# Region tiles and weight-split buffers start 0, 16, 32 or 48 bytes into their homes

## The chip, the cores and the metric

The kernel runs on one core of one Trainium2 chip. The metric is the device time in microseconds (us). The time of the kernel before is 2475.23 us, the median of 2 runs (2475.09 to 2475.36).

## What is computed

Two transformer blocks on 256 tokens of width 2048, all in float32 (the reference cut to its spine; the norms are RMS norms with a gain):

```python
def first_block(x, mem, ...):                      # x, mem: [1, 256, 2048]
    h = x
    h = h + hybrid_mixer(rms_norm(h, norm_mix), w_in, ..., w_out)      # w_in 2048 x 8272, w_out 2048 x 2048
    h = h + memory_cross_attention(rms_norm(h, norm_cross), rms_norm(mem, mem_norm), wq, wk, wv, wo, ...)
    h = h + sqrelu_mlp(rms_norm(h, norm_mlp), w_up, w_down)            # 2048 x 8192, 8192 x 2048
    return h

def hybrid_mixer(xn, w_in, ...):
    hq, hf, hi, hg, aq, ak, av, iq, ik, iw = split(xn @ w_in)
    y_h = hgrn2_group(hq, hf, hi, hg, ...)         # gated recurrence, 8 heads of 128
    y_a = dsa_group(aq, ak, av, iq, ik, iw, ...)   # top-64 causal attention, 8 heads of 128
    return concat(y_h, y_a) @ w_out

def sqrelu_mlp(hn, w_up, w_down):
    return square(relu(hn @ w_up)) @ w_down

def second_block(x, ...):
    x = x + neighbourhood_attention(rms_norm(x, ...), na_w_qkv, ..., na_w_o)   # 2048 x 6144, 2048 x 2048
    return x + sqrelu_mlp(rms_norm(x, ...), mlp_w1, mlp_w2)                    # 2048 x 8192, 8192 x 2048
```

## The kernel before

Every large product streams a weight matrix from HBM once. The stream is cut into chunks of 128 partitions x 1024 float32, two row tiles of 512 columns each. For a chunk, `emit_dma` loads `raw` on SP's queue (4 buffers); `emit_split` splits it exactly into two float32r parts: ScalarE (ACT) copies `raw` to `hi` (L374), VectorE (DVE) writes `lo = raw - hi` (L375); both have 4 buffers (`SPLIT_BUFS`), used in turn. The activations are split in the same way, so each product takes three matmuls: high x high, high x low, low x high. `emit_mm` issues them in one of two forms:

- **Transposed blocks** (`tr=True`, L408: the first part of the mixer's input projection and both up projections). The weights are stationary: 128 columns of `hi` or `lo` are loaded into TensorE, and 256 tokens of the activations `xT_hi` or `xT_lo` move through it. The output is feature by token.
- **Token blocks** (L415, L416, L417: all others). 128 tokens of the activations are stationary and 512 columns of `hi` or `lo` move (256 columns for the cross attention's values, `wv_x`). The activations are `xT_hi`/`xT_lo` for projections from the residual, and pairs of region tiles (`r` in the trace) for projections from something computed: the mixer's and the attentions' outputs, the normed memory, the squared ReLU.

A matmul with operands of float32r takes one weight load (LDWEIGHTS, on the row PEld of the trace) and one MATMUL (on PE). Nearly every matmul has a load of its own, and a trace shows the load of the next matmul begin when the present matmul begins.

Large intermediates live in nine regions of 8192 bytes per partition, made by `region(i, shape)` in pool `reg`: r0 to r7 of `[P, 8, 256]` or `[P, 2, 1024]`, and r8. Later stages take the same homes again: in the MLPs, group `g` of up columns uses r(2(g%4)) for its high and r(2(g%4)+1) for its low part; the neighbourhood attention keeps q and k in r0 to r3, v in r8 and its output in r4 to r7; the mixer's output lies in r0, r4, r5 and r6. Residual `X`, `xT_hi`, `xT_lo` and the identity (`cst`) are in pool `const`, and their addresses are not touched by any of these calls.

Work beside the stream (evacuations, softmax, the recurrence) is written as generators in lanes. Python clocks with estimated costs decide where in the program each of its steps goes; these clocks know sizes, not addresses.

GpSimd (POOL) issues 43 DMAs, among them two for each of the 16 bias tables (`relraw`) of the neighbourhood attention. The descriptors of these go through a scratch area at the start of SBUF, 16384 bytes per partition by default.

Addresses: the pools lie one behind the other, and every home is a multiple of 32 bytes. In the program as built, the first bytes of the operands of TensorE, modulo 64, are these (columns of 128 or 512 elements inside a tile are whole multiples of 64 bytes further on):

```
tile                         before   after
xT_hi, xT_lo, X, cst            0       0
raw (4 buffers)                32      32
hi, lo (buffers 0, 1, 2, 3)    32      32, 48, 0, 16
r0, r1                         32      32
r2, r3                         32      48
r4, r5                         32       0
r6, r7                         32      16
r8, wA, wE, wB                 32      32
```

Of the kernel before, what the change touches and what calls it, by code (L numbers as in the profile page):

```python
# [13 lines left out]
F32R = mybir.dt.float32r  # L14
# [8 lines left out]
P = 128  # L23
# [11 lines left out]
# columns of the transposed table of gains  # L35
# [20 lines left out]
class Block:  # L56
    """One block of output columns: w[kts, cols] against the stationary activations."""
# [7 lines left out]
class Act:  # L65
    """Transposed activations, each value split exactly into two float32r parts."""
# [9 lines left out]
def block_kernel(ctx: ExitStack, tc: "_tile.TileContext", a: dict, out: bass.AP, phases=ALL_PHASES):  # L76
# [27 lines left out]
    def region(i, shape, dtype=F32):  # L104
        return reg.tile(shape, dtype, tag=f"r{i}", name=nm(f"r{i}"))

    # ------------------------------------------------------------------ lanes of side work
    # Work beside the stream of weights is written as generators, each in a lane. The estimated clocks
    # below only order the program: a stage goes out when the one before it should be done by the time
    # the tensor engine gets there, and when ACT and DVE aren't too far behind it.  # L110
# [102 lines left out]
    # ------------------------------------------------------------------ constants  # L213
# [19 lines left out]
    # ------------------------------------------------------------------ small arithmetic  # L233
    def rsqrt(lane, x, n, mul=1.0, out=None):
        """1/sqrt(x) * mul of a [P, n] tile: an integer first guess, then Newton's steps."""
# [17 lines left out]
    def make_rstd(lane, key, ss, want_sq=False):  # L253
        """ss: [P, 2 * 4] sums of squares, one per token half and column block."""
        v = vec
        m = st(f"mr{lane}", 2)
        v.tensor_reduce(m, ss.rearrange("p (t c) -> p t c", t=2), axis=AX.X, op=ALU.add)
        ms = const.tile([P, 2], F32, name=nm("ms"))
        v.tensor_scalar(ms, m, 1.0 / D, EPS, op0=ALU.mult, op1=ALU.add)
        if want_sq:  # L260
            r2 = const.tile([P, 2], F32, name=nm("rsq"))
            v.reciprocal(r2, ms)
            rstd_sq[key] = r2
        else:
            rstd[key] = rsqrt(lane, ms, 2, out=const.tile([P, 2], F32, name=nm("rstd")))
        mark(("rstd", key))
# [3 lines left out]
    def build_half(lane, ver, cb, gain, half):  # L270
        """Two feature tiles of the finished residual: transposed, with the gain, split in two."""
# [43 lines left out]
    def split_act(hi, lo, src, scale=None):  # L315
        """hi + lo = src * scale, exactly; src in PSUM or SBUF."""
# [9 lines left out]
    def product(dst, l, r, first=True, last=True):  # L326
        """dst (+)= l^T r; operands split in two parts take three products."""
# [10 lines left out]
    def split_gains(parts, ps, gains):  # L338
        """The same of two feature tiles in one PSUM bank, each with its own gain."""
# [6 lines left out]
    # ------------------------------------------------------------------ the stream of weights  # L346
    plan = []

# [21 lines left out]
    def emit_split(c):  # L370
        n = len(c.kts) * c.block.width
        c.hi = stream.tile([P, 1024], F32R, tag="hi", name=nm("hi"))
        c.lo = stream.tile([P, 1024], F32R, tag="lo", name=nm("lo"))
# [53 lines left out]
    # ------------------------------------------------------------------ evacuations  # L427
    def ev_tokens(dst, key, after=None):
        """dst[tt] = projection * rstd, one row per token."""
# [13 lines left out]
    def ev_heads(dstT, key, gain, after, mul=1.0, lane="E", factor=None):  # L443
        """Four heads of 128: RMS norm of each, transposed; dstT(pair) is [128, 2, 256].

        With factor, the norm is left to the scores: factor["ss"] holds the heads' sums of squares.
        """
# [61 lines left out]
    def softmax_rows(lane, groups, factor=None):  # L509
        """groups: (scores [P, n, w] in SBUF or PSUM, destination [P, n, w]); normalised rows.  # L510

        factor(group) is a [P, n] of positive factors that the scores still lack.
        """
# [72 lines left out]
    # ------------------------------------------------------------------ phase: mixer  # L586
    def mixer():
# [46 lines left out]
        # --- indexer  # L634
# [91 lines left out]
        # --- sparse attention heads  # L726
# [70 lines left out]
        # --- gated recurrence heads  # L797
# [78 lines left out]
        def levels(g, pl):  # L876
            """Scores of the recurrence, S^T[s, t] = sum_k q[t] k[s] prod(f, s < . <= t): pairs are met at
            the level where a block of 2b tokens holds s in its left and t in its right half; q carries the
            products from its half's start, k those to its half's end."""
# [47 lines left out]
            def right_pairs(b, ps):  # L927
                """The level's products, for the tokens in right halves alone."""
# [95 lines left out]
    # ------------------------------------------------------------------ attention of dense heads  # L1024
    def probs_pair(qT, kTt, h0, pT, keys, bias=None, lane="A", pl="A", factor=None):
        """Two heads: softmax(q k^T + bias), transposed into the two tiles pT()."""
# [42 lines left out]
    def values_pair(pT, V, vcol, oT_hi, oT_lo, oh, act_o, vkey):  # L1069
        """out^T of two heads from their transposed probabilities, split into the next operand."""  # L1070
# [14 lines left out]
    # ------------------------------------------------------------------ phase: cross attention  # L1085
# [98 lines left out]
    # ------------------------------------------------------------------ phase: squared-ReLU MLP  # L1184
# [47 lines left out]
    # ------------------------------------------------------------------ phase: neighbourhood attention  # L1232
# [85 lines left out]
    # ------------------------------------------------------------------ the program  # L1318
# [107 lines left out]
```

## Time and profile before

| | |
|---|---|
| time, median of 2 runs | 2475.23 us |
| span of the profiled execution | 2475.9 us |
| PE busy | 2459.3 us, 99% of the span, 14885 matmuls |
| PEld busy | 2186.8 us, 88% |
| DVE busy | 1455.8 us, 59% |
| ACT busy | 1136.8 us, 46% |
| POOL busy | 169.5 us, 7% |
| DMA queue of SP | 440.19 MB, 57.0% of 16 engines |

How to read it: a matmul's busy time runs from its start to its modelled end and overlaps that of the next one, so 99% only says that PE is never without work. What one matmul costs in a stream is the distance from its start to the next one's start. The profile gives it in two ways: starts in the view in order of time, and the chain of work that ended last, whose merged pieces give the time of a run of matmuls together with their count.

### The profile page before, as it was taken

To read this page: it belongs to the slowest core of one execution; us is meant where nothing else is said; L and a number is where in the kernel's file an instruction comes from. 1 tells how busy PE (TensorE), PEld (TensorE's weight loads), DVE (VectorE), ACT (ScalarE), POOL (GpSimd) and SP (SyncE) were. 2 spreads that over 40 slices of the span, in tenths; PEclk is the share of its full clock that TensorE was granted. 3 is DMA by queue.
4 is the path that set the end of the run, shared out by engine and by line. 5 is a ranking of instruction groups with operands and counts; after the bars stand their busy time and mean duration, and the time that the engine had idled before them with its cause. 6 is when DMAs were issued, how large, how long until landed. Compare 5 with 4: busy or idle time off the path is not lost.

```text
span 2475.9 us, 36932 instructions
## 1 busy us (share of the span) xinstructions
PE 2459.3 (99%) x14885; PEld 2186.8 (88%) x14885; DVE 1455.8 (59%) x1719; ACT 1136.8 (46%) x1465; POOL 169.5 (7%) x345
## 2 busy tenths in 40 slices
PE   8999999999999999999999999999999999999999
PEld 8779998888998899899898888888998899899897
DVE  5575666665655555555556566666655555555554
ACT  5455533465543444444444554554543444444443
POOL 1020012211000000000000312230000000000000
PEclk9999999999999999999999999999999999999999
DMA  7555545555556556566655656555556656566654
GB/s 225 162 172 161 151 145 156 193 177 167 170 178 198 193 182 194 187 194 191 189 187 174 196 169 179 167 186 180 179 180 195 195 180 196 188 194 188 190 187 167
DMA packets 235644, 449.40 MB, mean 182 GB/s; under 512 B 16321, under 2 KB 21057, under 8 KB 235473
## 3 DMA queue, kind: packets, MB, share of 16 engines
q1 hardware_dynamic: 232528, 440.19, 57.0%
q0 software_dynamic: 2368, 5.80, 1.0%
q8 instruction: 116, 1.90, 0.3%
q10 hardware_dynamic: 576, 1.05, 0.1%
q14 instruction: 56, 0.45, 0.1%
HBM read 444.83 MB, written 2.10 MB: 181 GB/s over the span
## 4 chain that ended last, share of the span: by engine, by line
PE 95%; POOL 1%; DMA 1%; DVE 1%; ACT 1%; issue 0%; SPq 0%; ACTq 0%; POOLq 0%; DVEq 0%
PE acc L408 34%; PE acc L415 19%; PE acc L416 19%; PE acc L417 19%; PE sdA L157 3%; PE sdE L157 2%; DMA raw<-in_w_in_dram 1%; DMA relraw<-in_rel_dram 0%; POOL rhB L157 0%; ACT hi L374 0%; DVE lo L375 0%; DMA wA<-in_mem_dram 0%; POOL rhD L157 0%; DVE wB L157 0%; POOL rhE L157 0%
## 5 line engine op out<-in xcount | busy, mean ns | idle before, releaser
L375 DVE TENSOR_TENSOR lo<-raw,hi 128x1024 fp32r<-128x1024 f32 (+1 forms) x835 | 1005.1, 1222 | 495.0 <-ACT hi L374 492.0
L374 ACT ACTIVATE hi<-raw 128x1024 fp32r<-128x1024 f32 (+1 forms) x835 | 867.7, 1056 | 799.5 <-PE acc L417 406.0
L408 PE MATMUL acc<-xT_hi,hi 128*128 128x256 f32 x2448 | 690.6, 282 | 0.0
L408 PE MATMUL acc<-xT_hi,lo 128*128 128x256 f32 x2448 | 688.3, 281 | 0.1
L408 PE MATMUL acc<-xT_lo,hi 128*128 128x256 f32 x2448 | 688.2, 281 | 0.0
L415 PE MATMUL acc<-hi,r 128*128 128x512 f32 (+1 forms) x1408 | 543.6, 386 | 0.7 <-ACT r L157 0.7
L417 PE MATMUL acc<-hi,r 128*128 128x512 f32 (+1 forms) x1408 | 541.5, 385 | 0.0
L416 PE MATMUL acc<-lo,r 128*128 128x512 f32 (+1 forms) x1408 | 541.4, 384 | 0.0
L408 PEld LDWEIGHTS acc<-xT_lo,hi 128*128 128x128 f32 x2448 | 461.2, 188 | 0.6
L408 PEld LDWEIGHTS acc<-xT_hi,hi 128*128 128x128 f32 x2448 | 461.2, 188 | 0.6
L408 PEld LDWEIGHTS acc<-xT_hi,lo 128*128 128x128 f32 x2448 | 461.2, 188 | 0.3 <-DVE lo L375 0.3
L417 PEld LDWEIGHTS acc<-hi,r 128*128 128x128 f32 x1408 | 264.5, 188 | 53.1 <-DVE r L157 0.4
L415 PEld LDWEIGHTS acc<-hi,r 128*128 128x128 f32 x1408 | 264.7, 188 | 52.3 <-ACT r L157 1.1
L416 PEld LDWEIGHTS acc<-lo,r 128*128 128x128 f32 x1408 | 264.7, 188 | 51.0
L415 PE MATMUL acc<-hi,xT_hi 128*128 128x512 f32 x736 | 295.0, 401 | 0.0
L416 PE MATMUL acc<-lo,xT_hi 128*128 128x512 f32 x736 | 290.9, 395 | 1.4 <-DVE lo L375 1.4
L417 PE MATMUL acc<-hi,xT_lo 128*128 128x512 f32 x736 | 290.5, 395 | 0.0
L157 DVE SCALAR_TENSOR_TENSOR X<-acc,rsq,X 128x512 f32<-128x512 f32 x128 | 96.1, 751 | 147.0 <-PE acc L417 147.0
L415 PEld LDWEIGHTS acc<-hi,xT_hi 128*128 128x128 f32 x736 | 138.1, 188 | 33.8 <-issue 2.7
L417 PEld LDWEIGHTS acc<-hi,xT_lo 128*128 128x128 f32 x736 | 137.9, 187 | 33.7
L416 PEld LDWEIGHTS acc<-lo,xT_hi 128*128 128x128 f32 x736 | 138.2, 188 | 32.7 <-DVE lo L375 1.9
L157 DVE SCALAR_TENSOR_TENSOR wE<-acc,wE 128x512 f32<-128x512 f32 x64 | 44.3, 692 | 109.2 <-ACT wE L157 108.6
(175 smaller groups left out, 1121.9 us busy)
## 6 DMA issues: line engine op xcount, KB each, us to landing
raw<-in_mlp_w_dram SPq DMA_DIRECT2D x256, 512.0 KB, 4.2
raw<-in_w_up_dram SPq DMA_DIRECT2D x128, 512.0 KB, 3.9
raw<-in_w_down_dram SPq DMA_DIRECT2D x128, 512.0 KB, 4.3
raw<-in_w_in_dram SPq DMA_DIRECT2D x127, 512.0 KB, 3.9
raw<-in_na_w_qkv_dram SPq DMA_DIRECT2D x96, 512.0 KB, 4.2
raw<-in_w_out_dram SPq DMA_DIRECT2D x32, 512.0 KB, 4.2
raw<-in_na_w_o_dram SPq DMA_DIRECT2D x32, 512.0 KB, 4.1
raw<-in_wk_x_dram SPq DMA_DIRECT2D x8, 512.0 KB, 4.4
```

What stands on the lines that cost most here:

```text
L157: return f(*args, **kw)
L374: nc.scalar.activation(c.hi[:, :n], c.raw[:, :n], AF.Copy)
L375: nc.vector.tensor_tensor(c.lo[:, :n], c.raw[:, :n], c.hi[:, :n], op=ALU.subtract)
L408: nc.tensor.matmul(dst, l, r, start=first and i == 0 and o == 0, stop=last and i == 2, skip_group_check=True,)
L415: nc.tensor.matmul(dst, h, wh, start=first, stop=False)
L416: nc.tensor.matmul(dst, h, wl, start=False, stop=False)
L417: nc.tensor.matmul(dst, l, wh, start=False, stop=last)
```

## The change

`region` no longer makes a tile of the wanted shape; it takes a flat tile of 2064 elements (8256 bytes) and returns a view that begins `4 * (i // 2)` elements into it, so 0 bytes for r0 and r1, 16 for r2 and r3, 32 for r4 and r5, 48 for r6 and r7, and 0 for r8. `emit_split` takes tiles of 1040 elements (4160 bytes) and begins 0, 16, 32 or 48 bytes into them, by a counter that goes round with the four buffers; `hi` and `lo` of one chunk have the same start. `raw` is left as it is. To make room for the longer homes, the scratch area for GpSimd's DMA descriptors is set to 8192 bytes per partition. The other lines of the diff only take comments away; the kernel after has 11 lines more, so that its lines stand up to 11 further down (L374 is L385 there, L408 is L419).

```diff
     def region(i, shape, dtype=F32):
-        return reg.tile(shape, dtype, tag=f"r{i}", name=nm(f"r{i}"))
+
+        flat = reg.tile([P, 2064], dtype, tag=f"r{i}", name=nm(f"r{i}"))
+        n = 1
+        for d in shape[1:]:
+            n *= d
+        names = "abc"[: len(shape) - 1]
+        o = 4 * (i // 2) if i < 8 else 0
+        return flat[:, o : o + n].rearrange(
+            f"p ({' '.join(names)}) -> p {' '.join(names)}", **dict(zip(names, shape[1:])))
...
     plan = []
+    splits = [0]
...
     def emit_split(c):
         n = len(c.kts) * c.block.width
-        c.hi = stream.tile([P, 1024], F32R, tag="hi", name=nm("hi"))
-        c.lo = stream.tile([P, 1024], F32R, tag="lo", name=nm("lo"))
+        o = 4 * (splits[0] % SPLIT_BUFS)
+        splits[0] += 1
+        c.hi = stream.tile([P, 1040], F32R, tag="hi", name=nm("hi"))[:, o : o + 1024]
+        c.lo = stream.tile([P, 1040], F32R, tag="lo", name=nm("lo"))[:, o : o + 1024]
...
-    nc = _bacc.Bacc("TRN2", target_bir_lowering=False, num_devices=1)
+    nc = _bacc.Bacc("TRN2", target_bir_lowering=False, num_devices=1, dynamic_dma_scratch_size=8192)
```

No instruction moves. On each of the five engines the two built programs hold the same instructions in the same order with the same waits (14359 rows on PE, 1654 on DVE, 1287 on ACT, 846 on SP, 334 on POOL, all alike but for the line numbers). What differs is where operands lie: nearly every matmul, every split and every instruction that touches r2 to r7 gets another start address.

What this does to a matmul and the load that runs beneath it is best counted by pair: the start of the moving operand minus the start of the next stationary operand, modulo 64 bytes. Counted over the program (matmuls of float32r in the stream and beside it):

```
moving, next stationary                before            after
256 columns of xT, hi or lo (L408)     all at 32         0: 1828, 16: 1825, 32: 1828, 48: 1815
512 columns of hi or lo, xT            all at 32         0:  546, 16:  526, 32:  537, 48:  540
512 columns of hi or lo, r             nearly all at 0   0: 1021, 16:  975, 32: 1013, 48: 1081
```

## Rows read from the trace of the kernel before

**Rows 1.** The page, first lines: busy us (share of the span) xinstructions, by engine.
```profile
span 2475.9 us, 36932 instructions
PE 2459.3 (99%) x14885; PEld 2186.8 (88%) x14885; DVE 1455.8 (59%) x1719; ACT 1136.8 (46%) x1465; POOL 169.5 (7%) x345
```

**Rows 2.** Who waited for whom, engine PE: us in total, times, longest us.
```profile
PE sdE L157 <- DMA cst<-in_cst_dram: 2.9, 1, 2.9
...
PE acc L416 <- DVE lo L375: 1.4, 1, 1.4
```

**Rows 3.** Core: span and mean granted TensorE clock.
```profile
core 0: 2475.9 us, clock 1.000
```

**Rows 4.** Groups by line and form: shapes xcount, busy us, mean ns of one.
```profile
L408 PE MATMUL acc<-xT_hi,hi 128*128 128x256 f32 x2432 | 686.2, 282 | 0.0
L415 PE MATMUL acc<-hi,r 128*128 128x512 f32 x1344 | 525.3, 391 | 0.7 <-ACT r L157 0.7
L415 PE MATMUL acc<-hi,xT_hi 128*128 128x512 f32 x736 | 295.0, 401 | 0.0
L415 PE MATMUL acc<-hi,r 128*128 128x256 f32 x64 | 18.3, 285 | 0.0
```

**Rows 5.** In order of time, PE and PEld: start us, us, engine line op.
```profile
1000.12 0.28 PE L408 MATMUL acc<-xT_lo,hi 128*128 128x256 f32 x1
1000.12 0.19 PEld L408 LDWEIGHTS acc<-xT_hi,lo 128*128 128x128 f32 x1
```

**Rows 6.** The chain that ended last, in order of time: start us, us, what.
```profile
958.62 45.44 PE acc L408 x384
1047.63 45.44 PE acc L408 x384
```

**Rows 7.** In order of time, 512 columns against a region: first and last of 24.
```profile
1009.62 0.39 PE L416 MATMUL acc<-lo,r 128*128 128x512 f32 x1
...
1014.83 0.39 PE L415 MATMUL acc<-hi,r 128*128 128x512 f32 x1
```

**Rows 8.** In order of time, 512 columns against xT: first and last of 29.
```profile
1381.63 0.40 PE L417 MATMUL acc<-hi,xT_lo 128*128 128x512 f32 x1
...
1388.17 0.40 PE L415 MATMUL acc<-hi,xT_hi 128*128 128x512 f32 x1
```

**Rows 9.** In order of time, 256 columns against a region: first and last of 37.
```profile
591.81 0.28 PE L416 MATMUL acc<-lo,r 128*128 128x256 f32 x1
...
596.13 0.28 PE L416 MATMUL acc<-lo,r 128*128 128x256 f32 x1
```

**Rows 10.** The chain, the recurrence's products of 64 columns, levels b = 4, 8 and 16.
```profile
301.94 1.73 PE sdE L157 x16
...
309.40 1.73 PE sdE L157 x16
...
316.87 1.73 PE sdE L157 x16
```

**Rows 11.** Groups by form, the two splits of a chunk.
```profile
L375 DVE TENSOR_TENSOR lo<-raw,hi 128x1024 fp32r<-128x1024 f32 x831 | 1002.0, 1224 | 491.7 <-ACT hi L374 488.7 <-PE acc L417 0.3
L374 ACT ACTIVATE hi<-raw 128x1024 fp32r<-128x1024 f32 x831 | 865.0, 1058 | 795.6 <-PE acc L417 406.0 <-PE acc L408 311.6 <-issue 34.3
```

**Rows 12.** Who waited for whom, SP's queue: us in total, times, longest us.
```profile
SPq L365 <- DVE lo L375: 1989.8, 800, 8.0
```

**Rows 13.** Who waited for whom, all engines: the bias tables that GpSimd makes.
```profile
DVE wA L157 <- POOL relb L157: 6.5, 2, 5.2
```

**Rows 14.** The chain, where it goes through GpSimd's DMAs.
```profile
1545.21 3.95 DMA relraw<-in_rel_dram
...
1551.18 4.90 DMA relraw<-in_rel_dram
```

## The prediction

> **What bounds the kernel now.** I read the page first, then PE's waits, then the distance between matmul starts. The page gives PE as busy 99% of a span of 2475.9 us [rows 1]. The waits of PE say the same from the other side: its longest one is 2.9 us at the start, and in the whole program it waits 1.4 us for a `lo` part [rows 2]. The granted clock is 1.000, which is the 2.4 GHz level, throughout [rows 3]. So the time is the number of matmuls times the distance between their starts, and an edit counts by what it does to that distance.
>
> By clock alone a matmul of 256 columns would take 256 / 2.4 = 106.7 ns and one of 512 columns 213.3 ns. The stream is slower than that, and not evenly. Transposed blocks, 256 columns of `xT`: 45.44 us for 384, so 118.3 ns each [rows 6]. Token blocks against a region, 512 columns: from 1009.62 to 1014.83 us there are 23 distances, 226.5 ns each [rows 7]. The same matmul against `xT`: 28 distances in 6.54 us, 233.6 ns [rows 8]. The 256 columns of `wv_x` against a region: 36 distances in 4.32 us, 120.0 ns [rows 9].
>
> The pair to look at is rows 7 against rows 8. Both are the same instruction with the same `hi` and `lo` buffers moving, no wait in either, and the shape of the load is the same too. What differs is where the stationary operand starts: regions 32 bytes past a multiple of 64, as `hi` and `lo` are, and `xT` at a multiple. The load of the next weights begins with the present matmul [rows 5], so the two read SBUF together. I take it that the distance of their addresses, modulo 64, sets how much they hold each other up: 0 gives 226.5 ns at 512 columns and 120.0 at 256; 32 gives 233.6 and 118.3. Distances 16 and 48 do not occur in the stream before.
>
> **What the change does, part by part.** It removes and adds no instruction, moves none, and changes no wait; it changes start addresses. Four parts follow.
>
> First, the stream's pairs. The main groups are 3 x 2432 = 7296 transposed matmuls, 3 x 736 = 2208 of 512 columns against `xT`, 3 x 1344 = 4032 of 512 columns against regions, and 3 x 64 = 192 of 256 against regions [rows 4]. After, each of the first three has a quarter of its pairs at each distance 0, 16, 32, 48. Two of the four prices are known. For the other two I have bounds:
>
> - From below, a load with nothing in its way. The recurrence's products of 64 columns (plain float32, two passes each, so 16 records for 8 products) take 1.73 us for 16 loads, 108.1 ns each [rows 10]: 1.4 ns over a load of 128 columns at one per 0.833 ns (half of the 2.4 GHz clock, an assumption that 108.1 itself suggests). So 108.1 ns at 256 columns and, with the same 1.4 ns, 214.7 ns at 512.
> - From above, twice the worst excess seen. At 512 columns the worst excess over that floor is 233.6 - 214.7 = 18.9 ns, so 252.5; at 256 it is 120.0 - 108.1 = 11.9, so 131.9. No row says that 16 and 48 stay below this; I choose a factor of two because 0 and 32 differ by a factor of 1.6 at most (18.9 against 11.8).
>
> I take the middle of the two known prices for the unknown ones: 119.2 ns at 256 columns, 230.1 at 512. The reason is that the load passes over eight lots of 64 bytes while the moving operand passes over many more, so that they meet in every position whatever the start; 0 and 32 differ by only 7 ns, and nothing seen is near either bound. With it:
>
> - Transposed: the mean over the four becomes 119.2 instead of 118.3: 0.9 x 7296 = +6.2 us.
> - Against `xT`: 230.1 instead of 233.6: -3.5 x 2208 = -7.8 us.
> - Against regions: 230.1 instead of 226.5: +3.6 x 4032 = +14.3 us; the 192 of `wv_x` lose 0.8 x 192 = -0.2 us.
>
> Together +12.5 us. It is a small sum because the change mixes: the matmuls that had the dear distance get cheaper, those that had the cheap one dearer.
>
> The rows of the recurrence give one hint on 16. Their stationary operand starts at 32 modulo 64, the moving one at 48 (b = 4), 0 (b = 8) and 32 (b = 16), so distances of 16, 32 and 0; all three take 1.73 us [rows 10]. Distance 16 is therefore no trap in itself. But these streams are short and half as dense, so they hardly show any cost for 0 and 32 either, and the hint does not choose between the bounds.
>
> The Trainium skill speaks against my sum here. Its page "SBUF — State Buffer", section "Who interferes with whom", gives TensorE one read port for the moving operand and an independent one for weight loads, and says that it never waits on anyone; by that no start address matters, and the sum is 0. In the same page of the Trainium skill, section "Door 1: The DMA port swizzle", SBUF has lines of 16 bytes, and every shift here is a whole number of them. The trace does not agree with the first: 226.5 and 233.6 ns are one instruction with other addresses. The Trainium skill's page "TensorE: Matmul & The Clock Gate", section "Back-to-back issue gap", gives N/2.4 + 2.5 ns, which is 215.8 ns for 512 columns; no run of the stream here reaches it.
>
> Second, the splits. ACT writes `hi` in 1058 ns and DVE `lo` in 1224 ns per chunk [rows 11]. A chunk feeds 24 transposed matmuls (24 x 118.3 = 2.84 us) or 12 of 512 columns (12 x 226.5 = 2.72 us), and PE hardly ever waits for `lo`. DVE is busy 59%, so all of its work would have to take 1.7 times as long before it became the bound. I cost this at nothing. If a start between multiples of 32 doubled the 1224 ns of `lo`, DVE would have 0.59 x 2.72 + 1.22 = 2.83 us of work in such a chunk and become the bound by 0.1 us; no row hints at that.
>
> Third, the loads of `raw`. Their tiles keep their start modulo 64. SP's queue waits 1989.8 us for `lo` to release a buffer [rows 12], so loads come when splits let them, with room to spare: nothing.
>
> Fourth, GpSimd's scratch, half as large. If its DMAs had to wait for earlier ones to land, the two bias tables that are in the chain, 3.95 and 4.90 us [rows 14], would come later, by at most about as much again: +9 us. DVE waits only 6.5 us in all for these tables [rows 13]. I take 0 and keep +9 as a bound.
>
> **The sum.** The profiled span of 2475.9 us and the median of 2475.23 us are the same execution to 0.7 us, so I add to the median: 2475.2 + 12.5 = 2487.7 us, or +0.5%.
>
> **The rivals.**
>
> - *16 and 48 are free of conflict.* Speaks for it: 0 and 32 are the two distances at which both streams stand alike in 32 bytes, so they may be the bad ones; the free rows at 108.1 ns show that it can be had. Against: nothing at full density shows it. With 108.1 and 214.7 ns for both, transposed: (120.0 + 118.3 + 216.2) / 4 = 113.6, -4.7 x 7296 = -34.3 us; `xT`: (226.5 + 233.6 + 429.4) / 4 = 222.4, -11.2 x 2208 = -24.7 us; regions: 222.4, -4.1 x 4032 = -16.5 us. Sum -76 us: 2400 us, -3.0%. It is faster by 2% (-49.5 us) from about 70% of the way from the middle to free, 111.4 and 219.3 ns. Half of the way gives 2444 us, which is within 2%.
> - *16 and 48 are worse*, the other side. The place is the same, the load beneath a matmul. For it: a start at 16 or 48 also cuts lots of 32 bytes across, which nothing before does. At twice the worst excess: transposed (120.0 + 118.3 + 263.8) / 4 = 125.5, +7.2 x 7296 = +52.5 us; `xT` (226.5 + 233.6 + 505.0) / 4 = 241.3, +7.7 x 2208 = +17.0; regions +14.8 x 4032 = +59.7. Sum +129 us: 2604 us, +5.2%. It decides (+49.5 us) from about a third of the way, 123.2 and 237.2 ns.
> - *Addresses don't matter*, and rows 7 and 8 differ by something else that belongs to `xT` or to its stage. Then nothing moves: 2475 us. Against: rows 7 and 8 hold no waits and the same instructions. The Trainium skill's two ports, cited above, would give this time.
>
> **How the numbers follow.** Middle prices, up to a third of the way to either side: 0.48. Addresses don't matter: 0.12. 16 and 48 cheaper, but short of 2%: 0.10; cheaper and beyond 2%: 0.14. Dearer beyond 2%: 0.16. The time is that of the first, 2487.7 us. For the range I leave out the ends of the second and third: from 2420 us (77% of the way from the middle to the free prices) to 2540 us (45% of the way to double the excess); this holds the first, the no-effect case, the cheap half and a share of each end, some 0.8. Faster by over 2% has 0.14, slower by over 2% 0.16, within 2% 0.70; 2% is about what a measurement of this kernel can tell from no change.
>
> **What would show it.** In the profile after, runs of matmuls in the chain and in order of time give the distance for each buffer of `hi` and `lo`, and so for each pair; within one transposed block the price should change from chunk to chunk with a period of four. Right would be 120.0 at distance 0 in transposed chunks, 118.3 at 32, and something between or near at 16 and 48; `xT` blocks faster than 233.6 on the mean, region blocks slower than 226.5. Wrong would be the same distances everywhere as before (no effect of addresses), a price at 16 or 48 near 108 or above 123 ns, a price that goes by the moving or the stationary start alone and not by their distance, PE waiting for `lo`, or longer issues and landings of `relraw`.

## The result, and the profile after

The kernel after takes 2490.93 us (median of 2 runs, 2490.08 to 2491.78) against 2475.23 us: 1.0063 of the time before, interval 1.0046 to 1.0081. That is 0.6% slower. The interval leaves out 1, so there is a loss; it is within the 2% that the prediction called no change, and 3.2 us above the 2487.7 us forecast. The profiled span grew by 14.1 us, from 2475.9 us [rows 1] to 2490.0 us.

The page of the kernel after, its first lines (as in [rows 1]):

```profile
span 2490.0 us, 36932 instructions
PE 2473.6 (99%) x14885; PEld 2184.6 (88%) x14885; DVE 1455.9 (58%) x1719; ACT 1135.8 (46%) x1465; POOL 169.8 (7%) x345
```

The kernel after, PE's waits (as in [rows 2]):

```profile
PE sdE L165 <- DMA cst<-in_cst_dram: 2.9, 1, 2.9
...
PE acc L427 <- DVE lo L386: 2.0, 1, 2.0
```

The kernel after, the two splits of a chunk, groups by form (as in [rows 11]), of which the first is shown:

```profile
L386 DVE TENSOR_TENSOR lo<-raw,hi 128x1024 fp32r<-128x1024 f32 x831 | 1002.0, 1224 | 497.6 <-ACT hi L385 494.4 <-PE acc L428 0.3
```

PE is as full as before and waits as little: 11.9 us in all against 12.4 (2.0 us for a `lo` part, 1.4 before). A `lo` part takes the same 1224 ns wherever its operands begin. The mean granted clock is 0.999, short of 1.000 by one stretch right behind the 2.0 us wait: for 3.4 us the granted clock was 0.50, the 1.2 GHz level. The kernel after, in order of time on PE, six distances apart:

```profile
1566.44 0.63 PE L428 MATMUL acc<-hi,xT_lo 128*128 128x512 f32 x1
...
1569.00 0.60 PE L428 MATMUL acc<-hi,xT_lo 128*128 128x512 f32 x1
```

That is 0.43 us from start to start where 0.23 is usual, for eight matmuls: some 1.5 us of the 14.1. The rest lies in the distance from one matmul's start to the next at the full clock.

The kernel after, the chain that ended last, in order of time (start us, us, what; as in [rows 6]): transposed blocks of the first up projection.

```profile
871.76 44.99 PE acc L419 x384
...
961.32 44.99 PE acc L419 x384
...
1050.65 44.99 PE acc L419 x384
...
1140.31 45.16 PE acc L419 x384
```

384 transposed matmuls took 45.44 us before [rows 6]; now 45.03 on the mean of these four, 117.3 ns each instead of 118.3. Between the end of one such block and the start of the next stand 192 matmuls of 512 columns against regions: (961.32 - 871.76 - 44.99) / 192 = 232.1 ns, then 230.9, then 232.7 (before 226.9 by the same rows). Transposed matmuls became cheaper and region matmuls dearer.

The kernel after, in order of time on PE (start us, us, engine, line, op): five starts 24 matmuls apart, in a transposed block.

```profile
964.02 0.28 PE L419 MATMUL acc<-xT_hi,hi 128*128 128x256 f32 x1
...
966.87 0.28 PE L419 MATMUL acc<-xT_hi,hi 128*128 128x256 f32 x1
...
969.68 0.28 PE L419 MATMUL acc<-xT_hi,hi 128*128 128x256 f32 x1
...
972.40 0.28 PE L419 MATMUL acc<-xT_hi,hi 128*128 128x256 f32 x1
...
975.27 0.29 PE L419 MATMUL acc<-xT_hi,hi 128*128 128x256 f32 x1
```

Four chunks with `hi` and `lo` at 32, 48, 0 and 16: 2.85, 2.81, 2.72 and 2.87 us for 24 matmuls, so 118.8, 117.1, 113.3 and 119.6 ns. Same instructions, no wait; only the buffer changes.

The kernel after, the same view: 48 distances of 512 columns against `xT` (as in [rows 8]).

```profile
1378.48 0.39 PE L426 MATMUL acc<-hi,xT_hi 128*128 128x512 f32 x1
...
1389.71 0.39 PE L426 MATMUL acc<-hi,xT_hi 128*128 128x512 f32 x1
```

11.23 us / 48 = 234.0 ns, against 233.6 before: no change, since starts are printed to 10 ns, which is 0.2 to 0.4 ns in a price over 48 to 24 distances.

To see how much of the 14.1 us this is, I took the mean of all start-to-start distances under 420 ns in the trace, by form. The means also hold the few ends of blocks and the 192 narrow region matmuls, so they stand a little off the prices in a steady run; what counts is how they differ between kernels.

| | matmuls | before, ns | after, ns | difference, us |
|---|---|---|---|---|
| transposed | 7344 | 118.86 | 118.05 | -6.0 |
| against `xT` | 2208 | 235.38 | 235.67 | +0.6 |
| against regions | 4224 | 222.75 | 227.21 | +18.9 |
| sum | | | | +13.5 |

The span moved by +14.1. The eight starts at the lower clock are over 420 ns apart and so not in these means; with +1.5 us for them and -0.5 for the waits the account comes to 14.5.

### The profile page after: what moved, and what is told of

The parts are those of the page before. It is cut to its first block, busy times and chain, and to the rows that moved or that the text cites. A ratio compares the mean times of both kernels' runs of the same rounds, so it can differ in the third digit from the quotient of the medians.

```text
span 2490.0 us, 36932 instructions
## 1 busy us (share of the span) xinstructions
PE 2473.6 (99%) x14885; PEld 2184.6 (88%) x14885; DVE 1455.9 (58%) x1719; ACT 1135.8 (46%) x1465; POOL 169.8 (7%) x345
## 4 chain that ended last, share of the span: by engine, by line
PE 95%; POOL 1%; DVE 1%; DMA 1%; ACT 1%; issue 0%; SPq 0%; ACTq 0%; POOLq 0%; DVEq 0%
PE acc L419 33%; PE acc L426 19%; PE acc L428 19%; PE acc L427 19%; PE sdA L165 3%; PE sdE L165 2%; DMA raw<-in_w_in_dram 1%; DMA relraw<-in_rel_dram 0%; POOL rhB L165 0%; ACT hi L385 0%; DVE lo L386 0%; POOL rhD L165 0%; DVE wB L165 0%; DVE wA L165 0%; POOL rhE L165 0%
## 5 line engine op out<-in xcount | busy, mean ns | idle before, releaser
L385 ACT ACTIVATE hi<-raw 128x1024 fp32r<-128x1024 f32 (+1 forms) x835 | 866.9, 1055 | 816.8 <-PE acc L428 432.5
L419 PE MATMUL acc<-xT_hi,hi 128*128 128x256 f32 x2448 | 690.1, 282 | 0.0
L419 PE MATMUL acc<-xT_lo,hi 128*128 128x256 f32 x2448 | 687.4, 281 | 0.0
L419 PE MATMUL acc<-xT_hi,lo 128*128 128x256 f32 x2448 | 687.1, 281 | 0.1
L426 PE MATMUL acc<-hi,r 128*128 128x512 f32 (+1 forms) x1408 | 550.5, 391 | 0.7 <-ACT r L165 0.7
L428 PE MATMUL acc<-hi,r 128*128 128x512 f32 (+1 forms) x1408 | 548.5, 390 | 0.0
L427 PE MATMUL acc<-lo,r 128*128 128x512 f32 (+1 forms) x1408 | 547.0, 388 | 0.0
L419 PEld LDWEIGHTS acc<-xT_hi,hi 128*128 128x128 f32 x2448 | 461.6, 189 | 0.7
L419 PEld LDWEIGHTS acc<-xT_lo,hi 128*128 128x128 f32 x2448 | 461.4, 188 | 0.7
L419 PEld LDWEIGHTS acc<-xT_hi,lo 128*128 128x128 f32 x2448 | 461.6, 189 | 0.3 <-DVE lo L386 0.3
```

What stands on the lines that cost most here:

```text
L385: nc.scalar.activation(c.hi[:, :n], c.raw[:, :n], AF.Copy)
L419: nc.tensor.matmul(dst, l, r, start=first and i == 0 and o == 0, stop=last and i == 2, skip_group_check=True,)
L426: nc.tensor.matmul(dst, h, wh, start=first, stop=False)
L427: nc.tensor.matmul(dst, h, wl, start=False, stop=False)
L428: nc.tensor.matmul(dst, l, wh, start=False, stop=last)
```

## The experiments

The prediction rested on one reading: the price of a matmul goes by the start of its moving operand minus the start of the next stationary one, modulo 64. "Distance" below is this difference (it is counted modulo 512 here, so that a smaller period can be seen). The rival that no address matters had already fallen with the period of four above. What was open: whether the shifts of 16 to 48 bytes make the loss or something that comes with them, and what the true period is.

Two things besides the shifts differ in the kernel after: its homes are 64 bytes longer than a multiple of 4096 or 8192, and the scratch area is halved.

### The longer homes without the shifts

```diff
-        o = 4 * (i // 2) if i < 8 else 0
+        o = 0
...
-        o = 4 * (splits[0] % SPLIT_BUFS)
+        o = 0
```

(an edit of the kernel after, in `region` and in `emit_split`)

> The kernel after with every start set back to the home's first byte: homes of 4160 and 8256 bytes and the smaller scratch area stay, so all stream and region tiles start at 32 modulo 64 as before, but the homes are no longer alike modulo 512 (before all at 32 modulo 512). Theory D, that of the prediction (a price for each distance modulo 64 between the moving and the next stationary operand): all pairs as before, 2475 us, 226.5 ns for 512 columns against regions. Theory H (the low price against regions belongs to operands that are alike modulo 512 or more, and longer homes end that): regions near 231 ns, +4.5 x 4032 = +18 us, transposed blocks unchanged at 118.3, so about 2493 us. Theory M (neighbours in a row with unlike starts cost): 2475 us, as D.

Measured: 2492.37 us, 1.0065 of before (1.0049 to 1.0082), span 2488.9 us. Its chain:

```profile
961.34 45.32 PE acc L419 x384
...
1051.18 45.37 PE acc L419 x384
```

Regions (1051.18 - 961.34 - 45.32) / 192 = 231.9 ns, transposed 118.0. With every start at its old place modulo 64 the regions cost as much as in the kernel after: the longer homes are enough for the loss. Modulo 64 these addresses are those of the kernel before, so a period of 64 can't be right. In the program as built, the 64 extra bytes spread the distances of the region matmuls, which all were 0, over 0, 64, 128 and 192 modulo 256, about a thousand pairs each.

### The shifts without the spread

```diff
-        flat = reg.tile([P, 2064], dtype, tag=f"r{i}", name=nm(f"r{i}"))
+        flat = reg.tile([P, 2176 if i < 8 else 2048], dtype, tag=f"r{i}", name=nm(f"r{i}"))
...
-        c.hi = stream.tile([P, 1040], F32R, tag="hi", name=nm("hi"))[:, o : o + 1024]
+        c.hi = stream.tile([P, 1152], F32R, tag="hi", name=nm("hi"))[:, o : o + 1024]
```

(`lo` likewise: homes are multiples of 512 bytes, and the shifts of the kernel after stay)

> The kernel after with homes of 4608 and 8704 bytes (r8: 8192), so that all homes are alike modulo 512 (32) and only the starts of 0, 16, 32 and 48 bytes differ. Theory D: as the kernel after, 2491 us. Theory H: if it is the spread of the homes that costs, regions go back to 227 to 228 ns, -4.5 x 4032 = -18 us: about 2473 us. Theory M: as after, 2491 us, regions near 232 ns.

Measured: 2483.35 us, 1.0026 (1.0017 to 1.0036), span 2481.8 us. Its chain:

```profile
958.36 44.97 PE acc L419 x384
...
1047.48 44.97 PE acc L419 x384
...
1136.96 44.97 PE acc L419 x384
```

Transposed 117.1 ns, regions 230.0 and 231.8. The time lies between the two that were expected, 2473 and 2491 us. So the shifts alone make the regions nearly as dear as the longer homes alone do, and get more of it back from the transposed blocks (the table of sums further down). In the kernel after the two do not add up. My reading, which no run tests by itself, is that both mix the distances of the regions, and once those are mixed, another mixing changes little.

### Everything further on: 32 and 224 bytes

An unused tile ahead of the stream's pool moves the stream, the regions and the smaller pools together; `xT` stays. The region distances stay 0, those with `xT` change.

```diff
+    const.tile([P, 8], F32, name="gap")
     nc.sync.dma_start(out=cst, in_=a["cst"])
```

(an edit of the kernel before, 8 elements for 32 bytes and 56 for 224)

> The kernel before with an unused tile of 32 bytes at the head of the constants' pool's neighbours, so that raw, hi, lo and all regions move 32 bytes on, from 32 to 0 modulo 64, while xT stays at 0. Distances: 0 in all three groups of matmuls. Theory D by the prices of before: transposed 120.0 (+12 us), against xT 226.5 (-16 us), regions 226.5: 2472 us; by the price that the kernel after shows for transposed chunks at start 0 (115.1 ns, -23 us) and 226.5 against xT: 2436 us. Theory H (512 columns go by more than modulo 64): against xT still 233 ns, regions 226.5, transposed 115.1: about 2452 us. Theory M: as D with 115.1, 2436 us.

Measured at 32: 2462.76 us, 0.9942 (0.9927 to 0.9957), span 2459.9 us: faster than both kernels. Its chain, then two starts in order of time, 39 distances apart, against `xT`:

```profile
950.43 45.23 PE acc L409 x384
...
1039.18 45.23 PE acc L409 x384
```

```profile
1375.04 0.39 PE L416 MATMUL acc<-hi,xT_hi 128*128 128x512 f32 x1
...
1383.96 0.39 PE L416 MATMUL acc<-hi,xT_hi 128*128 128x512 f32 x1
```

Transposed 117.8 ns (distance 192, before 224), `xT` 228.7 (distance 64, before 288), regions 226.7. The regions' addresses moved by 32 like all others and their price did not: it goes by the difference of the two starts, not by either alone. None of the expected times (2436, 2452, 2472 us) came.

Not all transposed blocks of this kernel agree. Early in the program, in the mixer's input projection, two blocks of 168 matmuls, both at distance 192 throughout, have two prices. In order of time on PE, 33 distances in the one and 35 in the other:

```profile
42.11 0.28 PE L409 MATMUL acc<-xT_hi,lo 128*128 128x256 f32 x1
...
45.99 0.28 PE L409 MATMUL acc<-xT_hi,lo 128*128 128x256 f32 x1
...
258.17 0.28 PE L409 MATMUL acc<-xT_lo,hi 128*128 128x256 f32 x1
...
262.14 0.28 PE L409 MATMUL acc<-xT_hi,hi 128*128 128x256 f32 x1
```

3.88 us / 33 = 117.6 ns and 3.97 us / 35 = 113.4 ns. Each block keeps its price from its first few matmuls to its end.

> The same with an unused tile of 224 bytes: hi, lo, regions and xT all start at 256 modulo 512 (32 and 256 before). Theory D: as the kernel with 32 bytes. Theory H: now xT too is alike modulo 512 with what moves, so against xT 226.5 ns instead of 233.6 (-16 us), and transposed blocks 115.1 (-23 us): about 2436 us, some 16 us under the kernel with 32 bytes. Theory M: the same as with 32 bytes.

Measured at 224: 2474.37 us, 0.9992 (0.9983 to 1.0002), span 2473.0 us. Its chain, then 24 distances against `xT`:

```profile
956.63 46.07 PE acc L409 x384
...
1046.25 46.07 PE acc L409 x384
```

```profile
1383.80 0.39 PE L416 MATMUL acc<-hi,xT_hi 128*128 128x512 f32 x1
...
1389.24 0.39 PE L416 MATMUL acc<-hi,xT_hi 128*128 128x512 f32 x1
```

All distances are 0 now. `xT` falls to 226.7 ns, which is what regions cost at 0, so [rows 8] differ from [rows 7] by nothing but the distance; transposed rise to 120.0, which is what the narrow region matmuls of [rows 9] cost at 0. The gain of the one and the loss of the other cancel, where some 2436 us had been expected from 115.1 ns in transposed blocks. But distances 0 and 192, alike modulo 64, cost 120.0 and 117.8 ns.

### One address moved by 64, two ways

```diff
+    reg.tile([P, 16], F32, tag="gap", name="gap")
     nc.sync.dma_start(out=cst, in_=a["cst"])
```

(an edit of the kernel before: all regions, and the smaller pools behind them, 64 bytes further on; the stream and `xT` stay)

> The kernel before with an unused tile of 64 bytes ahead of the regions: hi and lo stay at 32 modulo 512, all regions move to 96, so every 512-column matmul against a region has one and the same distance to the next stationary operand, -64 instead of 0 modulo 512. Theory S (what gives 226.5 ns is that the distance stays the same from matmul to matmul, whatever it is): regions near 227 ns, 2475 us. Theory H (distance 0 modulo 512 is the cheap one): regions near 230 to 233 ns, as the kernel with longer homes shows at this distance, +3.5 to 6.5 x 4032 = +14 to +26 us, 2489 to 2501 us. Theory D (modulo 64): 2475 us.

Measured: 2499.96 us, 1.009 (1.0073 to 1.0107), span 2498.1 us. Its chain:

```profile
963.48 45.44 PE acc L409 x384
...
1053.71 45.44 PE acc L409 x384
```

Transposed 118.3 as before; regions 233.3 ns at distance -64, that is 448 or 192 modulo 256. A period of 64 would have given 226.9, and so would the expectation that any distance is cheap as long as it stays the same (theory S).

The 256 columns of `wv_x` against a region went the other way. In order of time on PE, 20 distances:

```profile
588.90 0.28 PE L418 MATMUL acc<-hi,r 128*128 128x256 f32 x1
...
591.16 0.28 PE L417 MATMUL acc<-lo,r 128*128 128x256 f32 x1
```

2.26 us / 20 = 113.0 ns at distance 192, against 120.0 at 0 [rows 9].

```diff
         c.hi = stream.tile([P, 1024], F32R, tag="hi", name=nm("hi"))
+        if not gaps:
+            gaps.append(stream.tile([P, 16], F32, tag="gap", bufs=1, name="gap"))
         c.lo = stream.tile([P, 1024], F32R, tag="lo", name=nm("lo"))
```

(an edit of the kernel before: 64 bytes between the homes of `hi` and those of `lo`; the pools behind them, the regions' too, move on by 64 with `lo`)

> The kernel before with an unused tile of 64 bytes between the hi and the lo buffers: hi at 32 modulo 512, lo and the regions at 96. All starts stay at 32 modulo 64, but the distance against a region now changes inside each group of three matmuls: -64 (hi moving), 0 (lo), -64 (hi). Theory S: regions lose the steady 227 and go to about 231 ns, +4.5 x 4032 = +18 us, 2493 us, while the kernel with all regions 64 on stays at 2475. Theory H: a third of the matmuls at 0, two thirds at -64: some two thirds of what the kernel with all regions 64 on loses, 2484 to 2493 us. Theory D: 2475 us.

Measured: 2498.85 us, 1.0087 (1.0072 to 1.0102), span 2497.7 us. Its chain:

```profile
962.96 45.23 PE acc L411 x384
...
1053.17 45.23 PE acc L411 x384
```

Regions 234.3 ns. Two of three products (those with `hi` moving) are at 192 modulo 256, one at 0. Priced apart they would average (2 x 233.3 + 226.9) / 3 = 231.2; the measured 234.3 is 3.1 ns dearer, and dearer than 233.3 throughout. The time, too, is above all that was expected (2493 us at most). In the trace the `lo` products, the ones at 0, are followed by the next start after 237.6 ns on the mean, the `hi` products after 233.5. A matmul at distance 0 between two others does not get the price of a run at 0: **alternating distances cost something of their own.**

### The stream 16 bytes on

```diff
-        o = 4 * (i // 2) if i < 8 else 0
+        o = 0
...
-        o = 4 * (splits[0] % SPLIT_BUFS)
+        o = 4
```

(in the homes of multiples of 512 bytes, as above: every region distance is 16, every transposed one 208)

> Homes alike modulo 512 (4608 and 8704 bytes), all hi and lo 16 bytes into theirs, regions at their first byte: one distance of 16 modulo 512 for all matmuls against regions, 240 below xT. Theory S: regions 227 ns, transposed 117.5 to 119, about 2475 us. Theory H: regions 231 ns (the price of distance 16 where starts change from chunk to chunk), about +18 us: 2493 us. Theory D: the middle price for distance 16, 230 ns, +14 us, with transposed 119: 2494 us.

Measured: 2502.4 us, 1.0101 (1.0086 to 1.0117), span 2499.9 us. Its chain:

```profile
872.38 45.23 PE acc L419 x384
...
962.09 47.35 PE acc L419 x384
...
1053.92 45.23 PE acc L419 x384
```

Regions (962.09 - 872.38 - 45.23) / 192 = 231.7 ns at a uniform distance of 16. Transposed blocks have two prices, 117.8 and 123.3 ns (47.35 / 384), with the same addresses and the same instructions; 4 of 12 blocks are the slow kind, every third one. In a fast block two distances of 116 or 117 ns and one of 120 go round and round; in a slow one 116 or 117 and 130 ns come in turn, from its first matmuls to its last. As in the kernel 32 bytes further on, a block falls into one of two patterns at its start and stays in it. What it inherits from what ran ahead of it must matter; I did not find out what. The slow blocks, 5.5 ns x 384 x 4 = 8.4 us, are about what the time is above the expected 2493 to 2494 us.

### The period: 96, 160 and 416 further, and the regions 256 and 512 on

The edits are those above with another number: `const.tile([P, 24])`, `[P, 40]` and `[P, 104]` for 96, 160 and 416 bytes, `reg.tile([P, 64])` and `[P, 128]` for 256 and 512. The last also takes the kernel after's halved scratch area:

```diff
-    nc = _bacc.Bacc("TRN2", target_bir_lowering=False, num_devices=1)
+    nc = _bacc.Bacc("TRN2", target_bir_lowering=False, num_devices=1, dynamic_dma_scratch_size=8192)
```

> The kernel before with an unused tile of 96 bytes ahead of the stream: hi, lo and regions at 128 modulo 512, xT at 256, one distance of 128 between them throughout. Theory S: regions 227 ns; transposed blocks at a distance of 128 near 115 ns (the short block of 80 columns shows 114 to 116 at multiples of 128), -3.3 x 7296 = -24 us; against xT 227 to 229 ns, -9 to -14 us: 2437 to 2445 us. Theory D: as the kernel 32 bytes on, 2463 us.

Measured at 96: 2482.58 us, 1.0023 (1.0014 to 1.0032), span 2481.7 us. Chain, and 24 distances against `xT`:

```profile
960.53 46.08 PE acc L409 x384
...
1050.17 46.08 PE acc L409 x384
```

```profile
1383.70 0.40 PE L417 MATMUL acc<-lo,xT_hi 128*128 128x512 f32 x1
...
1389.28 0.39 PE L417 MATMUL acc<-lo,xT_hi 128*128 128x512 f32 x1
```

Transposed 120.0 at distance 128, `xT` 232.5 at 384. Expected were 2437 to 2445 us (one distance throughout) or 2463 (a period of 64); neither came.

> The kernel before with 160 unused bytes ahead of the stream: hi, lo and regions at 192 modulo 512, xT at 256; distances moving minus next stationary: 64 in transposed blocks, 448 against xT, 0 against regions. Theory H with prices that hold for a distance wherever it occurs: transposed 115.0 ns (as chunks of the kernel after show at 64), -3.3 x 7296 = -24 us; against xT 233.3 (as regions at 448), 0; 2452 us. Rival, prices depend on the row of matmuls they stand in (transposed chunks at a distance of 192 took 113.8 ns between other distances and 117.4 alone): transposed 117 to 120 alone, 2467 to 2488 us.

Measured at 160: 2471.72 us, 0.998 (0.9971 to 0.9989), span 2469.4 us.

```profile
956.25 45.23 PE acc L409 x384
...
1045.04 45.23 PE acc L409 x384
```

```profile
1383.82 0.40 PE L417 MATMUL acc<-lo,xT_hi 128*128 128x512 f32 x1
...
1389.42 0.40 PE L417 MATMUL acc<-lo,xT_hi 128*128 128x512 f32 x1
```

Transposed 117.8 at 64, `xT` 233.3 at 448. That is what the rival expected; the 115.0 that chunks at 64 show in the kernel after did not come in these blocks. As in the kernel 32 further on, some short blocks of the mixer's input projection take 113.3 ns, at the same distance.

> The same with 416 bytes: hi, lo and regions at 448, distances 320 in transposed blocks, 192 against xT, 0 against regions. Theory H with prices by distance alone: transposed 115.0 ns, -24 us, against xT unknown between 227 and 233.3, -14 to 0 us: 2437 to 2452 us. Rival: transposed 117 to 120 when alone, 2452 to 2488 us.

Measured at 416: 2471.85 us, 0.9983 (0.9973 to 0.9992), span 2468.5 us. The chain's transposed blocks are 45.23 us as at 160; against `xT`, 24 distances:

```profile
1383.84 0.40 PE L418 MATMUL acc<-hi,xT_lo 128*128 128x512 f32 x1
...
1389.44 0.40 PE L418 MATMUL acc<-hi,xT_lo 128*128 128x512 f32 x1
```

117.8 and 233.3 again: 256 bytes further, nothing changes, in either form.

> The kernel before with 256 unused bytes ahead of the regions: distance against regions 256 modulo 512, all else as before. If distances repeat after 256 bytes or a part of it: 226.9 ns, 2476 us. If only after 512 or more: 229 to 233 ns, +8 to +26 us, 2484 to 2502 us. Theory D (modulo 64): 2476 us.

Measured: 2476.33 us, 1.0 (0.999 to 1.0009), span 2475.2 us.

```profile
958.41 45.44 PE acc L409 x384
...
1047.42 45.44 PE acc L409 x384
```

Regions 226.9 ns at distance 256, as at 0. This kernel and the one with the regions 64 on differ by the length of one tile that nothing uses, and are 23.6 us apart.

> The kernel before with the scratch area of 8192 bytes and 512 unused bytes ahead of the regions: all starts as before modulo 512, every address 8192 lower and the regions 512 on. If distances repeat after 512 bytes and the smaller scratch costs nothing: 226.9 ns against regions, 2476 us. If the pattern is longer than 512: 229 to 233 ns, 2484 to 2502 us. If the scratch costs something, relraw takes longer to issue or land and the time is higher with 226.9 ns.

Measured: 2477.84 us, 1.0006 (0.9997 to 1.0016), span 2475.8 us, chain 45.44 and 226.9 ns as before. The bias tables, by the view of that tile (issue to landing in us: least, median, most), here:

```profile
DMA to landing us min/median/max: 2.8/3.7/5.6
```

and in the kernel after:

```profile
DMA to landing us min/median/max: 2.7/3.5/5.1
```

The median before is 3.8 us by the same view. The halved scratch area costs nothing that this run can tell.

### The prices, and the sums

Steady prices in ns, by distance modulo 256. The rows at 0 and 192 of 512 columns hold for regions and for `xT` alike. The second price at 64 and 192 of 256 columns is that of the cheap blocks; `wv_x` at 192 takes 113.0. The price at 16 is that of `wv_x` alone, the mean of its starts in the run with the stream 16 on.

| distance | 512 columns moving | 256 columns moving |
|---|---|---|
| 0 | 226.7 to 226.9 | 120.0 |
| 16 | 231.7 | 118.8 |
| 32 | 233.6 | not run |
| 64 | 228.7 | 117.8 or 113.3 |
| 128 | 232.5 | 120.0 |
| 192 | 233.3 | 117.8 or 113.4 |
| 208 | not run | 117.8 or 123.3 |
| 224 | not run | 118.3 |

At 256 columns 0 costs what 128 costs, and 64 what 192 costs; so it is the 512 columns that tell a period of 256 from one of 128.

And where each kernel's difference lies, by the whole-trace means of the first section, in us against before:

| kernel | transposed | `xT` | regions | sum | span moved |
|---|---|---|---|---|---|
| after | -6.0 | +0.6 | +18.9 | +13.5 | +14.1 |
| longer homes, no shifts | -2.0 | +0.5 | +17.6 | +16.1 | +13.0 |
| shifts, homes of 512s | -8.0 | -3.2 | +16.4 | +5.2 | +5.9 |
| all 32 further | -7.5 | -8.6 | -0.3 | -16.3 | -16.0 |
| all 224 further | +12.2 | -12.2 | -0.1 | -0.2 | -2.9 |
| regions 64 on | -0.1 | +0.6 | +24.2 | +24.6 | +22.2 |
| stream 16 on | +6.1 | -0.2 | +18.4 | +24.4 | +24.0 |
| `lo` 64 on | -3.9 | -1.6 | +29.1 | +23.7 | +21.8 |
| all 96 further | +9.6 | -2.0 | +0.1 | +7.8 | +5.8 |
| all 160 further | -5.1 | 0.0 | +0.2 | -4.8 | -6.5 |
| all 416 further | -5.3 | 0.0 | +0.3 | -5.0 | -7.4 |
| regions 256 on | 0.0 | 0.0 | 0.0 | 0.0 | -0.7 |

Every line closes to about 3 us, so the distance between matmul starts carries every difference that is larger than that.

## Why the prediction was right, and where it was not

**What bounds the kernel: right.** PE's waits did not grow, the `lo` parts kept their 1224 ns, and nearly the whole difference is in the distances of matmuls; the 1.5 us at the lower clock are what the prediction did not have. The splits, the loads and the scratch area were rightly costed at nothing; the halved area was run with the regions 512 bytes on and the rest of before, and took 1.0006 of the time (0.9997 to 1.0016).

**Addresses matter, by their difference: right.** Everything 32 or 224 further leaves the regions at 226.7 to 226.8 ns; the regions alone 64 further take 233.3. The rival that addresses don't matter would have given 2475 us and one price in every chunk. The rule of the Trainium skill weighed there, that a matmul's moving operand and the weight load read through independent ports (page "SBUF — State Buffer", section "Who interferes with whom"), does not agree with these runs as the prediction took it, that no start address matters: by that the regions 64 on and 256 on would take the same time, and they are 23.6 us apart. The issue gap that the prediction takes from the Trainium skill's page "TensorE: Matmul & The Clock Gate", section "Back-to-back issue gap", is given there for a matmul by itself; that no run of the stream reaches it says nothing for or against it.

**"I take it that the distance of their addresses, modulo 64, sets how much they hold each other up": the step that failed.** The period is 256. Distances 0, 64, 128 and 192 are one case modulo 64 and cost 226.9, 228.7, 232.5 and 233.3 ns at 512 columns. The rows of before could not show it: their regions were all at 0 and their `xT` pairs all at 32 modulo 256, one value of each class. I took two points for a period. Nor does the distance set the price alone: the same distance gave 117.8 and 113.4 ns in blocks of one run.

**The longer homes, costed at nothing, are enough for nearly the whole loss.** The table of pairs modulo 64 counts them as no change. They alone move the span by 13.0 us and the regions by +17.6; with the shifts on top it is 14.1 and +18.9. The shifts alone, in homes of whole multiples of 512 bytes, move the span by 5.9.

**The terms.** Each is off, by -12.2, +8.4 and +4.8 us, and the sum, +12.5 forecast and +13.5 measured, is right because these cancel. That is luck:

- Transposed: predicted +6.2 us, measured -6.0. The mixed price was taken as 119.2 ns, the mean of 120.0 and 118.3; the chain shows 117.3. Distances of 64 and 192 at 117.8 or 113.4 were not in the two rows I averaged; the chunks at 113.3 in the kernel after stand at 64 modulo 256.
- `xT`: predicted -7.8 us, measured +0.6. The mixed price was taken as 230.1 and is 234.0. Distance 32 was taken as the dear one of two, and it is one of several. After, the pairs stand at 32, 144, 192 and 240 modulo 256. Steady rows give 233.6 at 32 and 233.3 at 192; 144 and 240 were run in no steady row, but their distances in the trace after have medians of 233 and 234. So mixing brings nothing.
- Regions: predicted +14.1 us with `wv_x`, measured +18.9. Again 230.1 was taken; the rows show 230.9 to 232.7. The plain mean of the steady prices at 0, 64, 128 and 192 is (226.9 + 228.7 + 232.5 + 233.3) / 4 = 230.4 ns, which explains 3.5 of the 5.0 ns that the longer homes alone cost; their distances are these four. I put the other 1.5 ns (some 6 us over 4032) down to distances that change from one matmul to the next. The run with `lo` 64 on shows such a cost for one change, between 192 and 0; no run splits it off in the kernel after.

So what held was the structure: mix the cheap distance of the regions away, and lose. What did not hold was that every mixed price lies halfway between two known ones.

**The other rivals.** No steady price reached the free bound (108.1 and 214.7 ns): 16 at 512 columns is 231.7, and the cheapest rows of 256 columns, 113.0 to 113.4, stand at 64 and 192, not at 16 or 48. Nor did one reach the dear bound (131.9 and 252.5), though the slow transposed blocks at 208, with 123.3 ns, passed the 123.2 from which that rival would decide. They are 4 of 12 blocks.

**The signs that were named.** The period of four is there, but not with the prices named for it: 120.0 was to stand at distance 0 modulo 64, where the rows show 113.3. `xT` was to be faster than 233.6 and is 234.0. The regions were to be slower, and are.

**Left open.** No run shows why it is 256 bytes. That the load and the moving read hold each other up fits the rows, but no run takes the load away. In every uniform run the present and the next stationary operand start alike modulo 256, so that these runs don't tell which of the two counts; I took the next, because its load runs beneath the matmul [rows 5]. Why do the same addresses give 117.8 and 123.3 ns, or 117.8 and 113.4, in different blocks, and why don't region matmuls at 0 in mixed surroundings go back to 226.9? Both say that a matmul's price also depends on the ones ahead of it; no run here takes that apart. It may be worth doing: if all 7344 transposed matmuls took 113.4 instead of 117.8 ns, that would be some 32 us, an estimate from the two prices.

**A version that beats both.** Everything 32 bytes further on: 2462.76 us, 0.58% under the kernel before, by one tile of 32 bytes. It has the lowest sum in the table, and the prices say why. The same stream is stationary in transposed blocks and moving in the others, so the two distances are one number with opposite signs. From all at 0 to stream 64 past `xT`, the `xT` matmuls lose 2.0 x 2208 = 4.4 us and the transposed gain 2.2 x 7344 = 16.2: 11.8 us together, and the two runs (224 and 32 further on) are 11.6 us apart.

## What to carry to other kernels

In a stream where every matmul has a weight load beneath it, the start addresses of both operands are a tuning knob worth up to about 1% here, either way (0.9942 to 1.0101 of before). Count moving start minus next stationary start modulo 256 for each form, since one distance can be cheap for one form and dear for another. Find the cheap value by a run, and try a small unused tile ahead of a pool before anything cleverer. Padding a home by 64 bytes is a change of that knob even where no instruction changes, so it has a cost that must be priced like any other. And a period read from two points is not a period: before building a sum on one, ask which other periods the same rows allow.

## What the runs showed of the hardware that was not expected

- A float32r matmul of 512 columns costs 226.7 to 234.3 ns, one of 256 columns 113.0 to 123.3 ns in steady rows, at a granted clock of 1.000, by address distance, mix and what ran ahead.
- The price by distance repeats after 256 bytes: 233.3 ns at distances 192 and 448; 226.9 at 0 and 256.
- The order of prices is not the same in the two forms: distance 0 is the cheapest for 512 columns (226.9) and among the dearest for 256 (120.0); 192 is dear for 512 (233.3) and cheap for 256 (117.8, or 113.0 to 113.4).
- Alternating between a cheap and a dear distance is dearer than the dear one throughout: 234.3 against 233.3 ns.
- Addresses that do not change can give two prices: 117.8 and 123.3 ns in blocks of one run at distance 208, 117.6 and 113.4 ns in blocks of another at 192. A block keeps the one with which it starts.
- In the kernel after, TensorE waited 2.0 us for a `lo` part, and the granted clock then stood at 0.50 for 3.4 us, with starts 0.43 us apart instead of 0.23.
